# The second feed-forward weights split by casting and accumulating DMAs from GpSimd's queue

## The chip, the cores and the metric

The program runs on one core of one Trainium2 chip. The metric is the device time of one execution in microseconds (us). The engines are named as in the profile: PE (TensorE, with its weight loads shown apart as PEld), DVE (VectorE), ACT (ScalarE), POOL (GpSimd) and SP (SyncE, which here only issues DMAs).

## The reference

The program computes one layer of a decoder trunk for 512 tokens of 1024 channels, in float32. Cut to what matters:

```python
h = rms_norm(x, g_mix)
p = h @ w_in                       # 1024 x 7680, feeds three token mixers and three gates
y = [hgrn2_mix(...) @ w_branch[0], short_conv_mix(...) @ w_branch[1], spatial_gating_mix(...) @ w_branch[2]]
x = x + (sum of sigmoid(gate) * y) @ w_o          # 1024 x 1024
h2 = rms_norm(x, g_ffn)
x = x + square(relu(h2 @ w_ff1)) @ w_ff2          # 1024 x 4096, then 4096 x 1024
return rms_norm(x, g_final)
```

The second feed-forward weights are `w_ff2`. They reach the kernel as `w_2`, 32 blocks of 128 x 1024 float32, 512 KB each.

## The kernel before, in words

Every large product is done in three passes on PE. Each operand is written as a high part, which is the operand rounded to the type fp32r, and a low part, which is what the rounding left; `mm3` (lines 88 to 91) then adds high x high, high x low and low x high in one PSUM accumulator. So every block of weights must be split before PE can use it.

The work on PE is a list of units, run in the order of the list by the loop at line 858. A unit is 24 matmuls of 128 x 128 by 512 columns, plus what hooks add (`pre` hooks run before a unit's matmuls, `post` hooks after them). A unit that needs a new block of weights names a load. Loads are kept in one list with the unit ("slot") at which they are split, two units or more before their use.

For each load the loop does three things. `issue` (line 731) starts the DMA of a block into one of three `raw` buffers. At the load's slot `split_hi` (line 739) has ACT copy `raw` to the high part, and `split_lo` (line 749) has DVE subtract the high part from `raw` and write the low part. Four loads are issued ahead of the loop, and from then on each split is followed by one more issue; so a load is issued when the load two places before it is split. Most blocks go to the rotating buffers `wh` and `wl` (three of each). The blocks of `w_2` go to 16 fixed buffers `h0` to `h15` instead (`hslot`; block i takes buffers 2 x (i mod 8) and the next), since a block of `w_2` is used in four units.

All engines keep the order of the program in their queues. Within one unit that order is: `split_hi` for the loads of this slot; the evaluation of the unit before (`ev_...`, its first half); `split_lo`; the evaluation's second half; the other `pre` hooks; `issue`; the matmuls; the `post` hooks.

The feed-forward part begins with eight units that matter here; call them U0 to U7. U0 to U3 are the first four products with `w_1`, whose results stay in PSUM at first, because the row scale of the second norm is not known yet:

- At U0 the evaluation of the last output-projection unit (`ev_o`, line 609) ends with a POOL addition into the sum of squares `sgb` (line 625).
- At U1 `ffn_split` (line 635) splits that sum, on ACT and then DVE, and `ffn_ss` (line 639) multiplies it by ones on PE (lines 145 and 146), behind U1's matmuls.
- At U2 `ffn_rows` (line 643) makes the row scale `r2b`: a square root on ACT, a reciprocal on DVE, two products on POOL (lines 649 and 650), one more operation on DVE (line 652).
- At U3 `ffn_late` evaluates U0 to U2 (`ev_1`, line 660: DVE, ACT, ACT, DVE).

In the slots of these units stand, in the order of the list: U0: `w_1` block 2; U1: `w_1` block 3, `w_2` block 0; U2: `w_1` 4, `w_2` 1; U3: `w_1` 5, `w_2` 2; U4: `w_2` 3, `w_1` 6; U5: `w_1` 7; U6 and on: `w_2` 4 to 7. `w_1` block n is used in unit Un for n up to 7; `w_2` blocks 0 to 3 are first used in U8.

From U4 on the part repeats with a period of eight units (seven groups): four units with `w_1`, four with `w_2`, and in its slots two loads of `w_1`, four of `w_2`, two of `w_1`. The four blocks of `w_2` of one group are used in the last four units of the next group. The last four blocks are used in the closing part (line 894 on), which starts three units after the last of them is split.

Of the kernel before, what the change touches and what calls it, by code (L numbers as in the profile page):

```python
# [8 lines left out]
F32R = mybir.dt.float32r  # L9
U8 = mybir.dt.uint8  # L10
AF = mybir.ActivationFunctionType
ALU = mybir.AluOpType
# [24 lines left out]
def trunk_kernel(ctx: ExitStack, tc, xT, w_f, w_t, w_bc, w_a, w_o, w_1, w_2, vecs, rows, w_sg, cst, lmask, out):  # L37
    nc = tc.nc
# [5 lines left out]
    dve, act, pool, pe = nc.vector, nc.scalar, nc.gpsimd, nc.tensor  # L44
# [3 lines left out]
    def nm(s):  # L48
        uid[0] += 1
        return f"{s}_{uid[0]}"  # L50

    def ct(shape, name, dt=F32):
        return cp.tile(shape, dt, name=name, tag=name)

    def xslot(i, dt):
        return rp.tile([P, S], dt, tag=f"x{i}", name=nm("x"))

    def zslot(i, dt):
        return rp.tile([P, S], dt, tag=f"z{i}", name=nm("z"))

    def hslot(i, dt):
        return rp.tile([P, 2 * S], dt, tag=f"h{i}", name=nm("h"))

    def acc():
        return pa.tile([P, S], F32, tag="acc", name=nm("acc"))

    def f(ap):
        return ap.bitcast(F32)

    def tt(e, o, a, b, op):  # L70
        return e.tensor_tensor(out=o, in0=a, in1=b, op=op)  # L71

    def raw():
        return wp.tile([P, 2 * S], F32, tag="raw", name=nm("raw"))
# [18 lines left out]
    def cs(k, n=P):  # L93
        return slice(k * n, (k + 1) * n)

    # constants
    vec = ct([P, V_N], "vec")
    cons = ct([P, C_N], "cons")
    ident = cons[:, C_ID:C_ID + P]
# [12 lines left out]
    def tmp(w=S, dt=F32):  # L112
        return wp.tile([P, w], dt, tag="tmp", name=nm("tmp"), bufs=6)

    def rsqrt_cols(src, n, inv, eps, dst):
        """dst[:, :n] = (src * inv + eps) ** -0.5"""
        a = wp.tile([P, 4], F32, tag="ra", name=nm("ra"), bufs=4)
        dve.tensor_scalar(out=a[:, :n], in0=src, scalar1=inv, scalar2=eps, op0=ALU.mult, op1=ALU.add)
        tt(pool, dst[:, :n], a[:, :n], mhalf[:, :n], ALU.pow)
# [49 lines left out]
    units = []  # L169
# [5 lines left out]
    loads, when = [], {}  # L175
# [14 lines left out]
            return a  # L190
        return unit(w_f[j], mm, ev)

    # recurrence: decays, keys, queries
    def ev_f(h, a):
        kk[h] = zslot(2 * h, F32)
        A[h] = zslot(2 * h + 1, F32)
        hs = [hslot(h * 4 + i, F32) for i in range(4)]
        names = ("QA", "t1", "QB", "y", "q", "R", "go", "att")
        d = {n: hs[i // 2][:, cs(i % 2, S)] for i, n in enumerate(names)}
        heads.append(d)  # L200
        fp = d["QA"]
        tt(dve, fp, a, rb, ALU.mult)
        act.activation(kk[h], fp, AF.Sigmoid, scale=-1.0)
        act.activation(d["t1"], fp, AF.Abs)
        pool.memset(d["att"], 0.0)
# [55 lines left out]
            dve.tensor_scalar(out=d["y"], in0=d["y"], scalar1=al[:, h:h + 1], scalar2=cl[:, h:h + 1], op0=ALU.add, op1=ALU.max)  # L261
            tt(dve, A[h], d["y"], d["t1"], ALU.add)

    # recurrence: interactions at distance scale m = 2 ** l
    def halves(ap, m):
        v = ap.rearrange("p (b two m) -> p b two m", two=2, m=m)
        if m == 1:
            v = v[:, :, :, 0]
            return v[:, :, 0], v[:, :, 1]
        return v[:, :, 0, :], v[:, :, 1, :]  # L270
# [51 lines left out]
            mk = lm[:, cs(l)].unsqueeze(1).to_broadcast([P, 4, P])  # L322
            dve.copy_predicated(v4(d["att"]), mk, v4(d["ps"]))

    # recurrence: blocks of 128 through the state
    def far_prep(pair):
        for h in pair:
            d = heads[h]
            act.activation(d["y"][:, :3 * P], d["R"][:, :3 * P], AF.Exp)
            act.activation(d["t1"][:, P:], A[h][:, P:], AF.Exp)  # L330
        for h in pair:
            d = heads[h]
            tt(dve, d["QA"][:, :3 * P], kk[h][:, :3 * P], d["y"][:, :3 * P], ALU.mult)
            tt(dve, d["QB"][:, P:], d["q"][:, P:], d["t1"][:, P:], ALU.mult)
# [39 lines left out]
    def mix_norm(pair):  # L374
        for h in pair:
            d = heads[h]
            ss, r = col4(), col4()
            for b in range(4):
                act.activation(d["QA"][:, cs(b)], d["ps"][:, cs(b)], AF.Square, accum_out=ss[:, b:b + 1])
            rsqrt_cols(ss, 4, 1.0 / P, EPS, r)  # L380
            d["r"] = r
# [17 lines left out]
            zt[0][h] = (zslot(2 * h, F32R), zslot(2 * h + 1, F32R))  # L399
            split(d["t1"], *zt[0][h])  # L400

    # spatial gate
    def v_mm(j):
        def mm(w):
            if j == 0:
                part["v"] = [acc() for _ in range(4)]
            a4 = part["v"]
            for k2 in range(2):
                k = 2 * j + k2
                for t in range(4):  # L410
                    mm3(a4[t], xh[k][:, cs(t)], xl[k][:, cs(t)], w[0][:, cs(k2, S)], w[1][:, cs(k2, S)], k == 0, k == KD - 1)
        return mm
# [19 lines left out]
    def v_norm():  # L432
        r = col4()
        rsqrt_cols(mv[:, :, 1], 4, 1.0, LN_EPS, r)
        for t in range(4):
            dve.tensor_scalar(out=vln[t], in0=vln[t], scalar1=mv[:, t, 0:1], scalar2=r[:, t:t + 1], op0=ALU.subtract, op1=ALU.mult)
# [42 lines left out]
        zt[2][g] = (zslot(16 + 2 * g, F32R), zslot(17 + 2 * g, F32R))  # L479
        split(part["sv", g], *zt[2][g])  # L480

    # short convolution
    def ev_cg(c, a):
        y = tmp()
        part["cy"] = y
        tt(dve, y, a, rb2, ALU.mult)
# [18 lines left out]
        yield  # L505
        tt(dve, lo, y, f(hi), ALU.subtract)

    # gates, branch outputs, merge
    def ev_gate(d, n, a):
        g = tmp()  # L510
        part[n] = g
        tt(dve, g, a, rb, ALU.mult)
        act.activation(g, g, AF.Sigmoid)
# [19 lines left out]
        tt(dve, mt[:, S:], part[0], f(mt[:, :S]), ALU.subtract)  # L533
        mg.append((mt[:, :S], mt[:, S:]))

    # order of the units of tensor work
    for h in range(NH):
        proj(4 + h, lambda a, h=h: ev_f(h, a))
    for h in range(NH):
# [57 lines left out]
        at(pre, 19 + g, sg_split, g)  # L597
    at(pre, 21, go_sig)

    # output projection, residual, second norm  # L600
    x2, x2h, x2l = [], [], []

    def reload_x():
# [37 lines left out]
        ones_mm(part["c2"], part["qh"], part["ql"])  # L641

    def ffn_rows():
        """-2 * (mean square + eps) ** -0.5, on every partition"""
        a, r, t = tmp(), tmp(), tmp()
        act.activation(r, part["c2"], AF.Sqrt, scale=1.0 / D, bias=eps_c)
        dve.tensor_scalar(out=a, in0=part["c2"], scalar1=1.0 / D, scalar2=EPS, op0=ALU.mult, op1=ALU.add)
        dve.reciprocal(r, r)
        tt(pool, t, a, r, ALU.mult)
        tt(pool, t, t, r, ALU.mult)  # L650
        part["r2b"] = ct([P, S], "rb2")
        dve.scalar_tensor_tensor(out=part["r2b"], in0=t, scalar=-3.0, in1=r, op0=ALU.add, op1=ALU.mult)
# [1 line left out]
    def ffn_late():  # L654
        return [ev_1(i, held[i]) for i in range(3)]

    # feed-forward
    hid = {}

    def ev_1(i, a):  # L660
# [48 lines left out]
    at(pre, f0 + 1, ffn_split)  # L709
    at(post, f0 + 1, ffn_ss)  # L710
    at(pre, f0 + 2, ffn_rows)
    at(pre, f0 + 3, ffn_late)
    for g in range(1, NG):
# [13 lines left out]
    raws, ws = {}, {}  # L727
    order = [x for s in sorted(when) for x in when[s]]
    issued = [0]

    def issue():
        if issued[0] < len(order):
            src, n, _ = loads[order[issued[0]]]
            r = raw()
            nc.sync.dma_start(r[:, :n], src)
            raws[order[issued[0]]] = r
            issued[0] += 1

    def split_hi(i):
        _, n, tiles = loads[i]  # L740
        if tiles:
            hi, lo = (hslot(t, F32R) for t in tiles)
        else:
            hi = wp.tile([P, 2 * S], F32R, tag="wh", name=nm("wh"))
            lo = wp.tile([P, 2 * S], F32R, tag="wl", name=nm("wl"))
        act.activation(hi[:, :n], raws[i][:, :n], AF.Copy)  # L746
        ws[i] = (hi, lo)

    def split_lo(i):
        n = loads[i][1]  # L750
        hi, lo = ws[i]
        tt(dve, lo[:, :n], raws.pop(i)[:, :n], f(hi[:, :n]), ALU.subtract)

    held = []
    with tc.manual_schedule():
        # warm the tensor engine's clock and the activation tables while the first loads run
        dve.memset(ones, 1.0)
        pool.memset(mhalf, -0.5)
        nc.scalar.dma_start(vec, vecs)
# [2 lines left out]
        warm = acc()  # L762
        for i in range(WARM):
            pe.matmul(warm[:, :P], ones, ones, start=True, stop=True)

        # x: load, scale by the gain, split, sum of squares; the recurrence's value rows, token-major
        xr = [zslot(k, F32) for k in range(KD)]
        rw = []
        for k in range(KD):
# [17 lines left out]
        for k in range(KD + 1):  # L787
            if k < KD:
                hi = xslot(2 * k, F32R)
                lo = xslot(2 * k + 1, F32R)  # L790
# [26 lines left out]
            if k == KD:  # L817
                cps = acc()
                col_sums(cps, sq_tot)
                rsqrt_cols(cps[:, :4], 4, 1.0 / D, EPS, rstd)  # L820
                dg = diag(rstd)
                dh = ones_hi(dg)
                dl = ones_lo(dg, dh)
# [3 lines left out]
            hi, lo = xh[j], xl[j]  # L827
# [6 lines left out]
            if j in (3, 5, 6):  # L834
                issue()
            if j == 5:
                split_hi(order[0])
                split_lo(order[0])
        issue()
        dve.tensor_copy(lm, lf[:, :7 * P])  # L840
        for t in range(4):
# [11 lines left out]
        for x in when[-1]:  # L853
            split_hi(x)
            split_lo(x)

        prev = None
        for i in range(len(units)):
            hooks = pre.get(i, [])
            todo = when.get(i, [])  # L860
            for x in todo:
                if x not in raws:
                    issue()
                split_hi(x)
# [12 lines left out]
            for x in todo:  # L877
                split_lo(x)
# [12 lines left out]
                fn(*a)  # L891
        prev[0](prev[1])

        # last group of the feed-forward, by token halves, and the final norm
        g = NG - 1
        n2 = S // 2

# [75 lines left out]
        warm = acc()  # L973
# [60 lines left out]
```

## Time and profile before

| what | value |
|---|---|
| runs | 857.92, 860.74, 861.56 us, median 860.74 us |
| profiled execution, first to last instruction (its span) | 859.3 us |
| PE busy | 847.2 us, 99% of the span |
| DVE, ACT, POOL busy | 473.6, 322.3, 140.4 us (55%, 38%, 16%) |
| DMA | 83.59 MB, 97 GB/s over the span |

The page gives one profiled execution; its span is the only time of it that is shown, and the runs are other executions of the same program. Busy is the time in which an engine executes instructions, not the time for which it is needed. Of two engines that are busy at once, the one whose next instruction others wait for sets the time; that is read from the chain of waits and from the timelines of the single engines, not from the shares.

### The profile page before, as it was taken

How to read it: one execution, taken by the hardware profiler on the slowest of the kernel's cores; microseconds unless marked ns; L12 is line 12 of the kernel's file. 1: busy time of each engine (PE TensorE's matmuls, PEld its weight loads, DVE VectorE, ACT ScalarE, POOL GpSimd, SP SyncE). 2: the span in 40 equal slices, each digit the busy share in tenths (PEclk: the TensorE clock that was granted, in tenths of full speed). 3: DMA queues.
4: the chain of work that ended last, by engine and by line, in shares of the span. 5: the costliest groups of instructions: out<-in, count | busy, mean ns of one | idle time of the engine just before them, and what ended most of it. 6: DMA issues, size and time to landing. Idle time of an engine off the chain costs nothing.

```text
span 859.3 us, 10105 instructions
## 1 busy us (share of the span) xinstructions
PE 847.2 (99%) x3990; PEld 706.8 (82%) x3990; DVE 473.6 (55%) x623; ACT 322.3 (38%) x491; POOL 140.4 (16%) x152
## 2 busy tenths in 40 slices
PE   8999899999999999999999999999999999999997
PEld 7888788888888888888888888888888888888896
DVE  7456989978564444544445458444444444444424
ACT  6567355354333232323223446232232323232222
POOL 4313455661210000000001310000000000000034
PEclk9999999999999999999999999999999999999999
DMA  8331222212122323232235234222223232322002
GB/s 302 118 99 50 84 88 75 74 50 98 50 75 86 110 86 111 86 96 100 86 110 208 92 131 149 96 98 98 98 98 98 98 98 98 98 91 90 17 1 99
DMA packets 26256, 83.59 MB, mean 97 GB/s; under 512 B 3040, under 2 KB 3424, under 8 KB 26208
## 3 DMA queue, kind: packets, MB, share of 16 engines
q1 hardware_dynamic: 26064, 82.91, 29.1%
q8 instruction: 31, 0.51, 0.2%
q14 instruction: 17, 0.14, 0.1%
q10 hardware_dynamic: 144, 0.03, 0.0%
HBM read 80.83 MB, written 2.10 MB: 97 GB/s over the span
## 4 chain that ended last, share of the span: by engine, by line
PE 91%; DVE 3%; ACT 3%; issue 2%; DMA 0%; SPq 0%; POOL 0%; DVEq 0%; ACTq 0%
PE acc L89 28%; PE acc L91 28%; PE acc L90 28%; PE acc L317 3%; PE acc L833 1%; DVE wl L71 1%; DVE h L71 1%; ACT h L248 1%; DVE h L261 0%; DMA z<-xT 0%; ACT wh L746 0%; ACT h L252 0%; PE acc L469 0%; PE acc L370 0%; DVE h L298 0%
## 5 line engine op out<-in xcount | busy, mean ns | idle before, releaser
L89 PE MATMUL acc<-x,wh 128*128 128x512 f32 x672 | 265.5, 395 | 0.0
L90 PE MATMUL acc<-x,wh 128*128 128x512 f32 x672 | 262.7, 391 | 0.0
L91 PE MATMUL acc<-x,wl 128*128 128x512 f32 x672 | 262.7, 391 | 0.0
L746 ACT ACTIVATE wh<-raw 128x1024 fp32r<-128x1024 f32 (+1 forms) x112 | 115.0, 1028 | 377.0 <-PE acc L90 247.4
L71 DVE TENSOR_TENSOR wl<-raw,wh 128x1024 fp32r<-128x1024 f32 (+1 forms) x118 | 151.4, 1284 | 24.9 <-ACT wh L746 24.8
L91 PEld LDWEIGHTS acc<-x,wl 128*128 128x128 f32 x672 | 126.2, 188 | 28.6
L89 PEld LDWEIGHTS acc<-x,wh 128*128 128x128 f32 x672 | 126.3, 188 | 26.5
L90 PEld LDWEIGHTS acc<-x,wh 128*128 128x128 f32 x672 | 126.3, 188 | 26.4
L71 DVE TENSOR_TENSOR z<-z,acc 128x512 f32<-128x512 f32 (+1 forms) x80 | 50.6, 634 | 109.8 <-PE acc L91 109.8
L89 PE MATMUL acc<-z,h 128*128 128x512 f32 (+1 forms) x288 | 105.5, 366 | 0.0
L90 PE MATMUL acc<-z,h 128*128 128x512 f32 (+1 forms) x288 | 105.2, 365 | 0.0
L91 PE MATMUL acc<-z,h 128*128 128x512 f32 (+1 forms) x288 | 105.2, 365 | 0.0
L71 POOL TENSOR_TENSOR tmp<-tmp,tmp 128x512 f32<-128x512 f32 (+1 forms) x27 | 31.5, 1166 | 218.6 <-DVE tmp L71 186.9
L662 DVE SCALAR_TENSOR_TENSOR tmp<-acc,rb 128x512 f32<-128x512 f32 x32 | 21.9, 690 | 76.0 <-PE acc L91 76.0
L71 DVE TENSOR_TENSOR tmp<-acc,rb 128x512 f32<-128x512 f32 x28 | 19.3, 691 | 80.5 <-PE acc L91 80.5
L89 PEld LDWEIGHTS acc<-z,h 128*128 128x128 f32 x288 | 54.3, 189 | 8.8
L90 PEld LDWEIGHTS acc<-z,h 128*128 128x128 f32 x288 | 54.3, 189 | 8.8
L91 PEld LDWEIGHTS acc<-z,h 128*128 128x128 f32 x288 | 54.3, 189 | 8.7
L917 POOL TENSOR_SCALAR z<-z,vec 128x256 f32<-128x256 f32 x12 | 5.8, 484 | 312.5 <-ACT tmp L911 312.5
L663 ACT ACTIVATE tmp<-tmp 128x512 f32<-128x512 f32 x32 | 20.1, 628 | 69.2 <-DVE tmp L662 69.2
L71 DVE TENSOR_TENSOR h<-raw,h 128x1024 fp32r<-128x1024 f32 x32 | 38.9, 1217 | 0.0
L89 PE MATMUL acc<-z,wh 128*128 128x512 f32 x96 | 37.8, 394 | 0.0
(184 smaller groups left out, 984.4 us busy)
## 6 DMA issues: line engine op xcount, KB each, us to landing
raw<-w SPq DMA_DIRECT2D x64, 512.0 KB, 3.3
raw<-w_f SPq DMA_DIRECT2D x52, 512.0 KB, 3.3
raw<-w_bc SPq DMA_DIRECT2D x8, 512.0 KB, 3.3
raw<-w_o SPq DMA_DIRECT2D x8, 512.0 KB, 3.3
z<-xT SPq DMA_DIRECT2D x15, 256.0 KB, 4.3
raw<-w_t SPq DMA_DIRECT2D x4, 512.0 KB, 3.3
raw<-w_a SPq DMA_DIRECT2D x8, 256.0 KB, 2.5
out<-x SPq DMA_DIRECT2D x8, 256.0 KB, 2.1
```

The costliest lines, as they stand in the source:

```text
L71: return e.tensor_tensor(out=o, in0=a, in1=b, op=op)
L89: pe.matmul(o, lh, rh, start=start, stop=False)
L90: pe.matmul(o, lh, rl, start=False, stop=False)
L91: pe.matmul(o, ll, rh, start=False, stop=stop)
L248: act.activation(d["t1"], d["t1"], AF.Exp, scale=-1.0)
L317: pe.matmul(ps[:, cs(b)], kl[:, cs(b)], qk[:, cs(b)], start=True, stop=True)
L662: dve.scalar_tensor_tensor(out=t, in0=a, scalar=0.0, in1=part["r2b"], op0=ALU.max, op1=ALU.mult)
L663: act.activation(t, t, AF.Square, scale=0.5)
L746: act.activation(hi[:, :n], raws[i][:, :n], AF.Copy)
L833: pe.matmul(a4[t], lh, rh, start=j == 0 and rnd == 0, stop=j == KD - 1 and rnd == 2)
L917: pool.tensor_scalar(out=xv, in0=xv, scalar1=vcol(V_GFIN + d), scalar2=0.0, op0=ALU.mult, op1=ALU.add)
```

## The change

For the 32 blocks of `w_2` (and for no others) `issue` no longer loads into `raw` from SP's queue. It takes the two `h` buffers at once, and a DMA in POOL's queue reads the block from memory and writes the high part, casting float32 to fp32r. At the slot, `split_hi` has ACT write minus the high part into the low buffer, and a second DMA in POOL's queue reads the block from memory again and adds it to the low buffer. `split_lo` does nothing for these blocks, so DVE's 32 subtractions go. The other hunks of the diff only take out comments.

```diff
     def issue():
         if issued[0] < len(order):
-            src, n, _ = loads[order[issued[0]]]
-            r = raw()
-            nc.sync.dma_start(r[:, :n], src)
-            raws[order[issued[0]]] = r
+            src, n, tiles = loads[order[issued[0]]]
+            if tiles:
+                hi, lo = (hslot(t, F32R) for t in tiles)
+                pool.dma_start(hi, src)
+                ws[order[issued[0]]] = (hi, lo)
+                raws[order[issued[0]]] = None
+            else:
+                r = raw()
+                nc.sync.dma_start(r[:, :n], src)
+                raws[order[issued[0]]] = r
             issued[0] += 1
 
     def split_hi(i):
-        _, n, tiles = loads[i]
+        src, n, tiles = loads[i]
         if tiles:
-            hi, lo = (hslot(t, F32R) for t in tiles)
+            hi, lo = ws[i]
+            act.activation(lo, f(hi), AF.Copy, scale=-1.0)
+            pool.dma_start(lo, src, accum_op=ALU.add)
+            return
         else:
...
     def split_lo(i):
         n = loads[i][1]
+        if loads[i][2]:
+            return
         hi, lo = ws[i]
         tt(dve, lo[:, :n], raws.pop(i)[:, :n], f(hi[:, :n]), ALU.subtract)
```

## Rows read from the trace of the kernel before

**Rows 1.** The page: busy time, share of span, instructions; 40 slices in tenths.
```profile
PE 847.2 (99%) x3990; PEld 706.8 (82%) x3990; DVE 473.6 (55%) x623; ACT 322.3 (38%) x491; POOL 140.4 (16%) x152
PEclk9999999999999999999999999999999999999999
```

**Rows 2.** The page: shares of the chain that ended last, by engine.
```profile
PE 91%; DVE 3%; ACT 3%; issue 2%; DMA 0%; SPq 0%; POOL 0%; DVEq 0%; ACTq 0%
```

**Rows 3.** Windows: length, busy us (instructions) of PE, PEld, DVE, ACT, POOL; clock, DMA share, GB/s.
```profile
495.00:539.00 44.00, 44.00 (x194) 36.11 (x193) 29.35 (x32) 25.05 (x32) 4.38 (x3) 1.00 0.46 144
561.00:605.00 44.00, 44.00 (x194) 36.25 (x194) 20.14 (x24) 12.88 (x16) 0.00 (x0) 1.00 0.29 96
605.00:649.00 44.00, 44.00 (x195) 36.27 (x194) 20.20 (x25) 12.88 (x16) 0.00 (x0) 1.00 0.29 96
```

**Rows 4.** Groups of instructions, 495 to 840 us: busy us, mean ns, idle before, releaser.
```profile
L71 DVE TENSOR_TENSOR h<-raw,h 128x1024 fp32r<-128x1024 f32 x32 | 38.9, 1217 | 0.0
L746 ACT ACTIVATE h<-raw 128x1024 fp32r<-128x1024 f32 x32 | 33.4, 1045 | 0.0
```

**Rows 5.** POOL in order of time, 495 to 530 us: start, length, line, tiles.
```profile
497.46 1.80 POOL L71 TENSOR_TENSOR sgb<-sgb,tmp 128x512 f32<-128x512 f32 x1 [3.70 <-ACT tmp L624]
514.19 2.67 POOL L71 TENSOR_TENSOR tmp<-tmp,tmp 128x512 f32<-128x512 f32 x2 [14.93 <-DVE tmp L648]
```

**Rows 6.** ACT in order of time, units U1 to U4.
```profile
501.58 1.04 ACT L746 ACTIVATE h<-raw 128x1024 fp32r<-128x1024 f32 x1
502.53 0.62 ACT L136 ACTIVATE tmp<-sgb 128x512 fp32r<-128x512 f32 x1
...
507.08 1.04 ACT L746 ACTIVATE h<-raw 128x1024 fp32r<-128x1024 f32 x1
508.14 1.28 ACT L646 ACT_TABLE_LOAD   x1
509.44 0.69 ACT L646 ACTIVATE tmp<-acc,eps_c 128x512 f32<-128x512 f32 x1
...
512.99 1.04 ACT L746 ACTIVATE h<-raw 128x1024 fp32r<-128x1024 f32 x1
...
521.98 1.05 ACT L746 ACTIVATE h<-raw 128x1024 fp32r<-128x1024 f32 x1
524.08 1.06 ACT L746 ACTIVATE wh<-raw 128x1024 fp32r<-128x1024 f32 x1 [1.06 <-DMA raw<-w]
```

**Rows 7.** DVE in order of time, units U1 to U4.
```profile
503.99 0.68 DVE L71 TENSOR_TENSOR tmp<-sgb,tmp 128x512 fp32r<-128x512 f32 x1
...
510.77 3.34 DVE L648 RECIPROCAL tmp<-tmp 128x512 f32<-128x512 f32 x1
...
519.42 1.21 DVE L71 TENSOR_TENSOR wl<-raw,wh 128x1024 fp32r<-128x1024 f32 x1
...
525.23 1.22 DVE L71 TENSOR_TENSOR wl<-raw,wh 128x1024 fp32r<-128x1024 f32 x1
```

**Rows 8.** PE in order of time: end of U1, third matmul of U5, start of U6.
```profile
506.33 0.39 PE L146 MATMUL acc<-tmp,ones_r 128*128 128x512 f32 x1
...
523.49 0.39 PE L91 MATMUL acc<-x,wl 128*128 128x512 f32 x1
...
528.52 0.39 PE L89 MATMUL acc<-x,wh 128*128 128x512 f32 x1
528.75 0.39 PE L90 MATMUL acc<-x,wh 128*128 128x512 f32 x1
528.99 0.39 PE L91 MATMUL acc<-x,wl 128*128 128x512 f32 x1
```

**Rows 9.** ACT and DVE in order of time, in a later group; PE at the closing part.
```profile
566.74 1.06 ACT L746 ACTIVATE wh<-raw 128x1024 fp32r<-128x1024 f32 x1 [15.42 <-PE acc L90]
568.89 1.04 ACT L746 ACTIVATE h<-raw 128x1024 fp32r<-128x1024 f32 x1
...
579.88 1.04 ACT L746 ACTIVATE h<-raw 128x1024 fp32r<-128x1024 f32 x1
...
567.83 1.23 DVE L71 TENSOR_TENSOR wl<-raw,wh 128x1024 fp32r<-128x1024 f32 x1 [0.17 <-ACT wh L746]
...
823.67 0.28 PE L89 MATMUL acc<-z,h 128*128 128x256 f32 x1
```

**Rows 10.** DMA issues: tile, queue, count, KB each, median us from issue to landing.
```profile
raw<-w SPq DMA_DIRECT2D x64, 512.0 KB, 3.3
z<-xT SPq DMA_DIRECT2D x15, 256.0 KB, 4.3
h<-w_t SPq DMA_DIRECT2D x2, 256.0 KB, 5.9
```

**Rows 11.** The page: GB/s moved by the DMA engines in 40 slices.
```profile
GB/s 302 118 99 50 84 88 75 74 50 98 50 75 86 110 86 111 86 96 100 86 110 208 92 131 149 96 98 98 98 98 98 98 98 98 98 91 90 17 1 99
```

## The prediction

> **What bounds the kernel now.** I read the page's busy shares first, then the chain of waits, then windows over the feed-forward part, and last the timelines of the engines where that part begins. PE is busy 99% of the span at full granted clock [rows 1], and the chain that ended last is PE for 91% [rows 2]. In the feed-forward part no hole is left at all: in windows of 44 us PE is busy 44.00 us, at clock 1.00, with 194 or 195 matmuls in each [rows 3]. So nothing that DVE, ACT or a queue does there is on the path, and the change, which lies in that part alone, can take time away only by making PE's own matmuls quicker. It can add time wherever it makes PE wait. The question is which margins it uses up.
>
> **What goes.** DVE loses 32 subtractions of 1217 ns, 38.9 us [rows 4]. DVE is busy 20 of 44 us in a later group [rows 3], all of it beside PE, so this is worth 0. The 32 loads of `w_2` leave SP's queue and the three `raw` buffers, so the loads of `w_1` start earlier; no PE instruction waits for them, worth 0. ACT keeps its 32 instructions: the copy of 1045 ns [rows 4] now reads the high buffer instead of `raw`. I cost it the same.
>
> **What comes.** 64 DMAs in POOL's queue, 32 that cast and 32 that accumulate, and two new waits: ACT's copy waits for the cast DMA, and the accumulating DMA waits in POOL's queue for that copy. Queued behind the first are ACT's splits of `w_1`, the square root and the evaluations; behind the second are the next cast DMA and, in U2, the two POOL products of `ffn_rows`.
>
> *In the six later groups* this has room. The first cast DMA of a group waits only for the `h` buffers, which PE leaves at about 561.5 us (the ACT instruction of the second unit starts at 566.74 [rows 9], one unit of 24 x 0.229 = 5.5 us later than that). ACT copies at 568.89, 7.4 us later. The third cast DMA is queued behind the accumulation that follows this copy, at about 569.9, and is wanted at 579.88 [rows 9], 10 us later. The results are used a group later, or three units (16 us) later in the last one. I cost these groups at 0 while a DMA lands in under about 8 us and the queue keeps its pace.
>
> *In the first group* they stand in a chain, because the loads come two to a slot and POOL and ACT also make the row scale. Let La to Ld be the times from POOL's turn to landing of the cast DMAs of blocks 0 to 3, and g the time that POOL spends on an accumulating DMA before it turns to the next.
>
> - Block 0's cast DMA is issued at U0 behind POOL's addition, which ends at 497.46 + 1.80 = 499.26 [rows 5].
> - It lands La later; ACT's copy takes 1.04 [rows 6]; the accumulating DMA takes g; block 1's cast DMA lands Lb later; ACT copies again, 1.04.
> - Only then does ACT come to its table load and square root, 2.01 (508.12 to 510.13 [rows 6]). The reciprocal on DVE ends 3.98 after that (514.11 [rows 7]), and POOL's two products 2.75 later (516.86 [rows 5]).
> - Block 2's cast DMA is issued in U2 after these hooks, so it stands behind both products. It lands Lc later, ACT copies, 1.04, the accumulation takes g, block 3's cast DMA lands Ld later, ACT copies, 1.04. (ACT's six evaluation instructions fit into g + Ld.)
> - Behind that copy stands ACT's split of `w_1` block 6. From its start to the end of DVE's low part a split takes 569.06 - 566.74 = 2.32 [rows 9].
>
> The fixed terms are 499.26 + 1.04 + 1.04 + 2.01 + 3.98 + 2.75 + 1.04 + 1.04 + 2.32 = 514.48. U6 wants this low part at its third matmul, 528.99 [rows 8]; before, it was there at 525.23 + 1.22 = 526.45 [rows 7]. So PE waits La + Lb + Lc + Ld + 2g - 14.5 us, if that is positive. What PE loses there is never given back, since there is no hole behind it.
>
> No row shows a cast or accumulating DMA or POOL's queue, so I bound them. Below: the plain 512 KB load from SP's queue, 3.3 us [rows 10], since the same bytes come from the same memory, and g = 0: 13.2 - 14.5, no wait. Above: 6.6 for each, two such transfers end to end, which exceeds the 5.9 of loads in a crowd [rows 10], and g = 1.8, a POOL instruction here [rows 5]: 26.4 + 3.6 - 14.5 = 15.5 us. I take 3.8 for a cast DMA by itself, halfway between 3.3 and the 4.3 of the reload of x [rows 10], since the size is that of the 3.3 row but the queue is POOL's and the data are cast. I add 1.6, half of 3.3, to Lb and Ld, which follow an accumulating DMA into the same engines. And g = 1, near the middle of its bounds. The sum is 3.8 + 5.4 + 3.8 + 5.4 + 2.0 - 14.5 = **5.9 us**.
>
> The same chain has two earlier ends. `ffn_split` on ACT and DVE is then done at 499.26 + 3.8 + 1.04 + 0.62 + 0.75 = 505.5, before PE wants the second half at 506.33 [rows 6 to 8]: no wait while La stays under 4.6. The low part of `w_1` block 5 was done at 520.63 for 523.49 [rows 7, 8], 2.9 us of margin, against a square root that ends 503.35 + La + Lb + g - 510.13 = 3.4 us later: about 0.6 of the 5.9 would be seen at U5, the rest at U6. These are parts of the same total, not additions.
>
> The Trainium skill, DMA: Bandwidth & Descriptors, section on the anatomy of one DMA on the SWDGE (gpsimd) path, fits a DMA from that queue as 2.0 us plus the bytes over 436 GB/s. As an estimate that makes 3.2 us for 512 KB, close to the 3.3 of the plain queue; with the same additions the wait would be 3.5 us instead of 5.9. No run here shows POOL's queue yet. Against the change, Collectives: The Full Stack says (stop 4 and the comparison of reduce-scatter) that an add in the DMA path costs not its arithmetic but a second source read; by that the accumulating DMA moves twice its size, which speaks for the addition to Lb and Ld.
>
> The profiled execution has a span of 859.3, so it becomes 865.2. The median of the runs, 860.74, lies 1.4 above this span; the forecast for the median is 860.74 + 5.9 = **866.6 us**.
>
> **The rivals.**
>
> *Hidden.* If a cast DMA lands like a plain one and accumulation hardly delays the next, the sum of the six terms stays below 18.8 and PE waits less than 4.3 us. With 3.3 each and g = 1 it waits 0.7: 861.4. For it: the DMA engines are used at 0.29 to 0.46 in this part [rows 3]. Against it: it needs all four landings near their lower bound. Not slower, 861 to 865.
>
> *The queue sets the pace.* 64 DMAs from 499.3 to the closing part at 823.67 [rows 9] leave 5.07 us for each. If they don't overlap and each takes more than that, PE waits in every group. At 6.6 the last would land at 499.3 + 422.4 = 921.7, and with the closing 35.6 the span is 957, the median 959. Against it: in the first slice of the span the engines moved 302 GB/s [rows 11]; at that rate 512 KB take 1.7 us, and twice that for an accumulation makes 2.6 on average, half of the limit.
>
> *Faster.* The mechanism would be that PE's reads of SBUF are slowed by DVE's two-input subtractions, so that without the 32 of them the matmuls follow each other more closely. 0.5% needs 1.3% of the 329 us from U0 to the closing part. Against it: the matmuls at 528.52, 528.75 and 528.99 start 0.23 apart [rows 8], and the count per 44 us is 194 where DVE is busy 29 us and 194 where it is busy 20 [rows 3]. Price at most some 4 to 5 us: 856.
>
> **How the numbers follow.** The chain in the first group (2 to 16 us) gets 0.58, of which 0.53 above 4.3 us; hidden 0.31; the queue as the bound 0.07; faster 0.04, of which 0.03 beyond 0.5%. 0.5% is about what a measurement of this kernel can tell from no change. That makes slower 0.60, same 0.37, faster 0.03. The range goes from just below no change, 860.0, to 878.0, the upper bound of the chain (876.3) and a little; outside are most of the queue's case, the faster one and a tenth of the rest.
>
> **What would show it.** In the changed profile: PE has one hole near the start of U6 of some 5 us and perhaps a small one at U5, both ended by the low part of `wl`, and none in later groups; DVE has no instruction on `h` from `raw`; ACT waits for DMA at its first four copies into `h`; POOL's two products of `ffn_rows` start later than 514.19. The prediction fails if these landings total under 16.5 us with g, if holes recur every eight units, or if PE's matmuls change their spacing.

## The result, and the profile after

The changed kernel takes 871.76 us (median of 4 runs, 871.11 to 874.04), the kernel before 860.16 us in the same set (4 runs, 857.92 to 861.56). The ratio is 1.0133, 95% interval 1.0105 to 1.0160: slower by 11.6 us. The forecast was 866.6 us, slower by 5.9.

The page of the changed kernel, against [rows 1, 2]. Busy time and share of the span; PE, clock and DMA in 40 slices of 21.8 us; the chain by engine.

```profile
PE 853.2 (98%) x3990; PEld 710.4 (81%) x3990; DVE 439.1 (50%) x591; ACT 321.4 (37%) x491; POOL 184.7 (21%) x216
...
PE   9999899999999999999999997999999999999996
...
PEclk9999899999999999999999998999999999999998
DMA  8331222213122332333244256855555555553502
...
PE 86%; DVE 4%; ACT 4%; DMA 3%; issue 2%; POOL 0%; SPq 0%; DVEq 0%; POOLq 0%; ACTq 0%
```

DVE lost its 32 subtractions (623 to 591 instructions, 473.6 to 439.1 us), POOL has 64 more, ACT is where it was. DMA is now 3% of the chain. One slice in the middle of the feed-forward part is weak: PE's digit there is 7 and the clock's 8, where both were 9 before. (The fifth slice and the last, outside that part, have an 8 of the clock too, and 9 before.) Windows over that part show the same, against [rows 3]:

```profile
480.00:520.00 40.00, 40.00 (x177) 32.82 (x176) 16.80 (x17) 16.34 (x20) 10.23 (x8) 1.00 0.47 133
520.00:560.00 40.00, 33.70 (x132) 26.48 (x131) 17.10 (x24) 20.12 (x27) 11.09 (x14) 0.91 0.74 186
560.00:600.00 40.00, 40.00 (x177) 32.99 (x176) 14.37 (x19) 12.23 (x17) 5.69 (x8) 1.00 0.61 157
600.00:640.00 40.00, 40.00 (x177) 32.95 (x177) 14.26 (x18) 8.95 (x12) 4.80 (x7) 1.00 0.59 151
```

From 520 to 560 us PE runs 132 matmuls where a full window holds 177, and is idle for 6.3 us; before and after that it misses nothing. PE's timeline in that window, against [rows 8] (the third matmul of U5, the last of U5, and the first three of U6; the brackets give the idle time before, and what ended it):

```profile
527.18 0.50 PE L91 MATMUL acc<-x,wl 128*128 128x512 f32 x1 [2.29 <-DVE wl L71]
...
533.71 0.40 PE L91 MATMUL acc<-x,wl 128*128 128x512 f32 x1
537.59 0.50 PE L89 MATMUL acc<-x,wh 128*128 128x512 f32 x1 [3.48 <-ACT wh L755]
537.93 0.39 PE L90 MATMUL acc<-x,wh 128*128 128x512 f32 x1
538.85 0.72 PE L91 MATMUL acc<-x,wl 128*128 128x512 f32 x1 [0.53 <-DVE wl L71]
```

These are the two holes of the forecast, at U5 and U6, each ended by a split of `w_1`. The chain that leads to them is on POOL's and ACT's timelines. POOL, against [rows 5] (line 736 is the cast DMA, 750 the accumulating one):

```profile
498.70 1.80 POOL L71 TENSOR_TENSOR sgb<-sgb,tmp 128x512 f32<-128x512 f32 x1 [3.70 <-ACT tmp L624]
500.44 0.78 POOL L736 DMA_DIRECT2D h<-w  x1
505.66 0.89 POOL L750 DMA_DIRECT2D h<-w  x1 [4.45 <-ACT h L749]
506.22 0.90 POOL L736 DMA_DIRECT2D h<-w  x1
514.93 0.87 POOL L750 DMA_DIRECT2D h<-w  x1 [7.81 <-ACT h L749]
520.70 2.65 POOL L71 TENSOR_TENSOR tmp<-tmp,tmp 128x512 f32<-128x512 f32 x2 [4.90 <-DVE tmp L648]
523.30 0.60 POOL L736 DMA_DIRECT2D h<-w  x1
528.41 0.88 POOL L750 DMA_DIRECT2D h<-w  x1 [4.52 <-ACT h L749]
529.15 0.70 POOL L736 DMA_DIRECT2D h<-w  x1
```

ACT, against [rows 6] (line 749 is the copy into the low buffer):

```profile
504.28 1.06 ACT L749 ACTIVATE h<-h 128x1024 fp32r<-128x1024 f32 x1 [1.37 <-DMA h<-w]
...
513.57 1.06 ACT L749 ACTIVATE h<-h 128x1024 fp32r<-128x1024 f32 x1 [5.17 <-DMA h<-w]
514.65 1.28 ACT L646 ACT_TABLE_LOAD   x1
515.94 0.69 ACT L646 ACTIVATE tmp<-acc,eps_c 128x512 f32<-128x512 f32 x1
...
527.05 1.06 ACT L749 ACTIVATE h<-h 128x1024 fp32r<-128x1024 f32 x1 [9.47 <-DMA h<-w]
...
535.53 1.06 ACT L749 ACTIVATE h<-h 128x1024 fp32r<-128x1024 f32 x1 [3.87 <-DMA h<-w]
536.50 1.04 ACT L755 ACTIVATE wh<-raw 128x1024 fp32r<-128x1024 f32 x1
```

The four copies wait for the four cast DMAs, and each accumulating DMA waits in POOL's queue for the copy. PE loses speed too. In windows of 5 us the granted clock (the column after the engines) falls to 0.76 to 0.90 around the holes; the matmuls behind each hole start 0.43 us apart for about 3 us, which is the lower of the clock's two levels (1.2 GHz), and 0.23 apart before and after:

```profile
520.00:525.00 5.00, 4.89 (x22) 3.68 (x20) 2.19 (x4) 0.00 (x0) 3.12 (x3) 1.00 0.10 16
525.00:530.00 5.00, 2.81 (x10) 2.28 (x11) 2.80 (x4) 2.88 (x5) 1.43 (x2) 0.87 0.55 195
530.00:535.00 5.00, 4.10 (x14) 2.95 (x12) 2.00 (x4) 1.63 (x3) 0.00 (x0) 0.79 0.92 209
535.00:540.00 5.00, 1.89 (x5) 1.26 (x6) 2.43 (x4) 4.10 (x5) 1.96 (x3) 0.90 0.33 47
540.00:545.00 5.00, 5.00 (x18) 3.96 (x18) 2.47 (x4) 2.56 (x4) 0.00 (x0) 0.76 1.05 337
545.00:550.00 5.00, 5.00 (x24) 4.10 (x23) 1.99 (x3) 3.24 (x5) 2.85 (x4) 1.00 1.03 265
```

To compare stretches, I read the starts of U0, U8, the closing part and the first of PE's last four matmuls (line 149 before; "last PE" below) from PE's timeline of each profiled execution. Differences in us:

```
kernel            U0 starts  U0 to U8  U8 to closing  closing to last PE  last PE to end  span
before              495.11     44.40      284.16            28.51             7.16       859.34
after               496.34     54.73      284.18            28.51             8.51       872.27
first 4 plain       497.22     44.41      284.16            28.50             7.86       862.15
first 4 only        495.62     54.32      284.18            28.51             7.51       870.14
casts together      495.14     44.41      284.16            28.50             8.52       860.73
block 6 ahead       496.72     48.62      284.17            28.50             8.51       866.52
cast only           494.21     44.81      284.17            28.51             7.23       858.93
accumulate only     494.32     44.41      284.16            28.50             7.24       858.63
cast 2 early        494.69     47.47      284.17            28.51             8.51       863.35
holes filled        493.91     53.30      284.16            28.50             8.52       868.39
```

Of the 12.93 us between the two profiled executions 10.33 lie between U0 and U8. Counted as what PE's starts lose against their usual spacing of 0.23, these are 2.46 of waiting at U5, 1.72 of slow clock behind it, 3.65 and 0.80 of waiting at U6, and 1.69 of slow clock behind that. From U8 to the closing part, where 26 of the 32 blocks are split, nothing changes by more than 0.02 us. 1.35 lie behind the last matmuls, and 1.23 ahead of U0, where all these programs do the same work and still differ by up to 3.3; part of the 1.23 is the clock, which over 87 to 109 us was 0.92 before and 0.84 after.

### The profile page after: what moved, and what is told of

It is laid out like the page before. It is cut to its first block, busy times and chain, and to the rows that moved or that the text cites. A ratio compares the mean times of both kernels' runs of the same rounds, so it can differ in the third digit from the quotient of the medians.

```text
span 872.3 us, 10126 instructions
## 1 busy us (share of the span) xinstructions
PE 853.2 (98%) x3990; PEld 710.4 (81%) x3990; DVE 439.1 (50%) x591; ACT 321.4 (37%) x491; POOL 184.7 (21%) x216
## 4 chain that ended last, share of the span: by engine, by line
PE 86%; DVE 4%; ACT 4%; DMA 3%; issue 2%; POOL 0%; SPq 0%; DVEq 0%; POOLq 0%; ACTq 0%
PE acc L89 27%; PE acc L91 27%; PE acc L90 27%; PE acc L317 3%; DMA h<-w 2%; PE acc L844 1%; DVE wl L71 1%; DVE h L71 1%; ACT wh L755 1%; DMA z<-xT 1%; ACT h L248 1%; DVE h L261 0%; ACT h L252 0%; PE acc L370 0%; PE acc L469 0%
## 5 line engine op out<-in xcount | busy, mean ns | idle before, releaser
L750 POOL DMA_DIRECT2D h<-w x32 | 27.9, 871 | 173.0 <-ACT h L749 173.0
L71 DVE TENSOR_TENSOR z<-tmp,z 128x512 fp32r<-128x512 f32 x40 | 27.6, 690 | 35.6 <-ACT z L666 35.6
L749 ACT ACTIVATE h<-h 128x1024 fp32r<-128x1024 f32 x32 | 33.6, 1049 | 28.0 <-DMA h<-w 28.0
L736 POOL DMA_DIRECT2D h<-w x32 | 23.1, 732 | 91.1 <-PE acc L90 90.4
```

The source lines that it names most:

```text
L736: pool.dma_start(hi, src)
L749: act.activation(lo, f(hi), AF.Copy, scale=-1.0)
L750: pool.dma_start(lo, src, accum_op=ALU.add)
```

## The experiments

**Which blocks?** Two kernels split the 32 blocks between the old path and the new:

```diff
+    plain = {w2l[i] for i in range(NF) if i < 4}      # in the second kernel: i >= 4
...
-            if tiles:
+            if tiles and order[issued[0]] not in plain:
```

> Blocks 0 to 3 of w_2 take the old path (load into raw, copy on ACT, subtraction on DVE); the other 28 keep the two DMAs from POOL's queue. Chain theory (all the loss sits where the feed-forward part begins, U1 to U7): back to before, 859 to 862 us, no hole in PE after U0. Rival A (every DMA from POOL's queue costs PE a little, spread over all groups): 28/32 of the loss stays, about 870 us. Rival B (a fixed cost of using POOL's queue at the start or the end of the program): 861.5 to 863 us, with the excess outside the feed-forward part.

Measured: 861.83 us against 860.56 in the same set, ratio 1.0016 (1.0005 to 1.0026). U0 to U8 takes 44.41 us, as before, with 56 DMAs still in POOL's queue. This refutes the loss spread over all groups; the 1.3 us that stay are partly the 0.7 behind the last matmuls.

> The reverse: only blocks 0 to 3 of w_2 go by POOL's queue, the other 28 by the old path. Chain theory: nearly the whole loss, 869 to 872 us, with the two holes of PE at U5 and U6. Rival A: 4/32 of the loss, about 861.6 us. Rival B: 861.5 to 863 us.

Measured: 872.31 us, ratio 1.0132 (1.0118 to 1.0146). Four blocks of 32 carry the loss: U0 to U8 takes 9.92 us more than before, against 10.33 with all 32. The holes are the same two, as its waits of PE show (engine, tile and line, what it waited for: us in all, times, longest):

```profile
PE acc L89 <- ACT wh L758: 3.7, 1, 3.7
...
PE acc L91 <- DVE wl L71: 2.5, 2, 2.0
```

**Is it the order or the transfers?** Three kernels keep all 64 DMAs and change only where some instruction stands. First, the four cast DMAs of the first group are issued together at U0:

```diff
+                for x in ([w2l[j] for j in range(4)] if i == w2l[0] else [i]):
+                    if x not in ws:
...
+                        pool.dma_start(hi, loads[x][0])
```

> All 64 DMAs stay, but the four cast DMAs of blocks 0 to 3 are issued together at U0, so that none stands behind an accumulating DMA or behind the two POOL products of ffn_rows. Chain theory: the landings are no longer added up; the last lands by about 510 us, no wait of PE, 859 to 863 us. Rival C (POOL's queue is short of bandwidth where it meets the loads of w_1, so that the order does not matter): still 868 us or more, since four transfers then meet at once.

Measured: 862.61 us, ratio 1.0021 (1.0011 to 1.0032); U0 to U8 44.41 us, no hole. So bandwidth was not short: the same transfers, closer together, cost PE nothing. POOL's queue now reads as follows; all four casts stand ahead of the first accumulation and of the products:

```profile
499.24 2.39 POOL L739 DMA_DIRECT2D h<-w  x4
504.47 0.91 POOL L753 DMA_DIRECT2D h<-w  x1 [2.84 <-ACT h L752]
508.46 0.87 POOL L753 DMA_DIRECT2D h<-w  x1 [3.08 <-ACT h L752]
514.23 2.66 POOL L71 TENSOR_TENSOR tmp<-tmp,tmp 128x512 f32<-128x512 f32 x2 [4.90 <-DVE tmp L648]
```

Second, in U4's slot block 6 of `w_1` is split ahead of block 3 of `w_2`:

```diff
-    for i in range(GF):
+    for i in range(GF - 1):
         load_2(f0 + 1 + i, i)
...
             w1l[g * GF + 2 + j] = load(b0 + j, w_1[g * GF + 2 + j])
+            if g == 1 and j == 0:
+                load_2(b0, 3)
```

> Only the order in one slot is changed: block 6 of w_1 is split ahead of block 3 of w_2, so ACT's copy for U6 no longer stands behind the fourth cast DMA. Chain theory: the hole at U6 goes (3.65 and 0.80 us of waiting and 1.69 us of slow clock behind it), the hole at U5 stays (2.46 and 1.72): about 865.5 us. Rival C: 871 us, since the same transfers meet.

Measured: 866.43 us (863.96 to 868.30), ratio 1.0068 (1.0053 to 1.0083). The hole at U5 stays with 2.10 us, the one at U6 shrinks to 0.78, and U0 to U8 takes 4.22 us more than before. The expected 4.18 had 1.72 of slow clock in it; here the clock stayed at 1.00 and small waits at U6 and U7 made up the sum, so the total was met partly by chance.

Third, in U2 the cast DMA of block 2 is issued ahead of the two products of `ffn_rows`:

```diff
+            if i == f0 + 2:
+                for x in todo:
+                    issue()
             for fn, a in hooks:
```

> Only the place of one issue is changed: in U2 the cast DMA of block 2 is issued ahead of the two POOL products of ffn_rows. Chain theory: it lands some 5 us earlier and ACT's copy of it waits no more; the hole at U6 goes, the one at U5 stays: about 865.5 us. Rival D (the POOL products do not matter, the chain is all in the transfers): 870 to 872 us.

Measured: 865.77 us, ratio 1.0055 (1.0038 to 1.0072); U0 to U8 is 3.07 us longer than before. The hole at U5 is unchanged and the one at U6 is gone but for 0.19, again at clock 1.00:

```profile
525.52 0.51 PE L91 MATMUL acc<-x,wl 128*128 128x512 f32 x1 [2.28 <-DVE wl L71]
...
531.50 0.50 PE L91 MATMUL acc<-x,wl 128*128 128x512 f32 x1 [0.19 <-DVE wl L71]
```

So a POOL instruction of 1.3 us, twice, was a link of the chain, by its place in the queue.

**Which half?** One kernel keeps only the cast DMA (the low part comes from `raw` by DVE), one only the accumulating DMA (ACT makes the high part from `raw`, DVE writes its negative); the comments are added here:

```diff
+                pool.dma_start(hi, src)                 # cast only; the block goes to raw too
...
+            dve.tensor_scalar(out=lo, in0=f(hi), scalar1=-1.0, scalar2=None, op0=ALU.mult)
+            pool.dma_start(lo, loads[i][0], accum_op=ALU.add)   # accumulate only
```

> One half of the change: the high part is written by the cast DMA from POOL's queue; the low part comes from raw by DVE's subtraction as before, so there is no accumulating DMA and no ACT copy for w_2. Chain theory: a cast DMA no longer stands behind an ACT copy and an accumulation, so the landings overlap; no wait of PE, 859 to 862 us, although ACT is rid of 32 instructions (33 us) too. Rival (ACT's time matters): faster than before, below 857 us.

Measured: 861.91 us against 860.89, ratio 1.0012 (1.0001 to 1.0023). Not faster, though ACT has 32 instructions less.

> The other half: the high part is made as before from raw by ACT; DVE writes minus the high part, and the accumulating DMA from POOL's queue adds the block. ACT waits for no DMA of POOL's queue. Chain theory: no wait of PE, 859 to 862 us. Rival A (accumulating DMAs slow PE or the other loads in all groups): 864 us or more.

Measured: 860.28 us, ratio 0.9990 (0.9981 to 1.0000), as before. Neither half costs anything worth naming. The loss needs both: the accumulation that waits for ACT's copy, the copy that waits for a cast, and the next cast behind that accumulation.

These two also separate the engine time of the kinds, that is the time that a DMA's packets took, summed and divided by 16 engines. The DMA queues of the cast-only kernel (packets, MB, share of 16 engines' span; q0 is POOL's queue), and then of the accumulate-only one:

```profile
q1 hardware_dynamic: 26064, 82.91, 28.5%
q0 software_dynamic: 4608, 16.78, 6.0%
```

```profile
q0 software_dynamic: 4608, 16.78, 11.5%
```

A cast of 512 KB takes 0.060 x 858.9 / 32 = 1.61 us of all engines, about as long as a plain load (0.285 x 858.9 us for 82.91 MB, 1.55 us for 0.524 MB). An accumulation takes 0.115 x 858.6 / 32 = 3.09, though the queue counts the same 16.78 MB for it.

**The clock.** 30 matmuls whose results nobody uses are put in front of U5 (10) and U6 (20); the comment is added here:

```diff
+            for _ in range(fill):                       # {5: 10, 6: 20}
+                pe.matmul(a, x2h[0][:, :P], x2h[0], start=True, stop=True)
```

> The changed kernel with 30 extra matmuls of 512 columns whose results are overwritten: 10 at the start of U5 and 20 at the start of U6, 6.9 us of extra work at full clock, put into the two holes. If the clock falls because PE stood idle: it stays at 1.00 and 2.5 to 3.4 us come back, 868.4 to 869.3 us, in spite of the extra work. If the clock falls for another reason (the DMA engines at a share of 0.9 to 1.05 there): no gain, 871.5 to 874 us.

Measured: 870.90 us, ratio 1.0112 (1.0092 to 1.0133). In its profile the clock is 1.00 in every 5 us window from 520 to 550, although the DMA share rises to 1.14 there, and U0 to U8 takes 53.30 us, 1.43 less than in the changed kernel, in spite of the extra work:

```profile
530.00:535.00 5.00, 4.70 (x21) 3.57 (x19) 0.52 (x1) 1.75 (x2) 0.40 (x1) 1.00 0.46 140
535.00:540.00 5.00, 4.16 (x17) 3.15 (x18) 4.42 (x6) 3.62 (x6) 1.57 (x3) 1.00 0.79 170
540.00:545.00 5.00, 5.00 (x24) 4.09 (x23) 1.74 (x3) 2.46 (x4) 1.43 (x2) 1.00 1.14 372
```

That speaks for idleness, not DMA traffic, as what lowered it, and so does the casts-together kernel, in which PE has no hole and the clock is 1.00 from 500 to 515 us at a DMA share of 1.00. But the gain was expected at 2.5 to 3.4 us. The lines of the changed kernel above give the reason: the slow clock after the first hole (1.72 us) ran while PE would have waited for the second hole's release anyway, and only the slow matmuls after the second hole (1.69 us) reached the end. On the medians, from two sets of runs, the gain is 0.9 us, and the two intervals overlap (1.0092 to 1.0133, and 1.0105 to 1.0160 for the changed kernel), so they do not show it. Nor does every hole lower the clock: it did not fall behind the 2.28 us in the kernel with block 2's cast issued early, nor behind the 2.10 with block 6 ahead, but it fell behind 2.29 in the changed kernel and behind 1.99 with the first four blocks only. What decides between these stays open.

## Why the prediction was right, and where its size was off

**Right: the mechanism, the place and the free parts.** PE had no hole to give back and none was gained; the later groups cost 0 (U8 to closing, 284.16 and 284.18); DVE's 38.9 us were worth 0; the loss stands at U5 and U6 of the first group. The hole at U6 was ended first by the high part (3.48 us) and then by the low part (0.53), where the forecast named the low part alone. The prediction also passed over blocks 4 to 7, which are in neither its first group nor its six later ones: of the 28.0 us that ACT waits for casts in the changed kernel (eight waits), 8.1 are at these four. No PE instruction waited for them, so the 0 was right there by margins that had not been worked out.

**The chain, term by term.** POOL's addition ends at 500.50 here. The cast DMAs land 3.78, 7.35, 3.70 and 6.38 us after their turn (504.28, 513.57 from 506.22, 527.05 from 523.35, 535.53 from 529.15), and POOL passes each accumulation 0.88 and 1.04 after the copy's end. The formula gives 21.21 + 1.92 - 14.5 = 8.6. PE's third matmul of U6 would have started at 528.99 + 1.23 = 530.22 in this execution and started at 538.85: 8.63 late. The fixed terms were all as read from before.

**Wrong: the size of Lb and Ld.** La and Lc were taken as 3.8 and were 3.8 and 3.7. Lb and Ld, the casts behind an accumulating DMA, were taken as 5.4 (an addition of 1.6) and were 7.35 and 6.38. The addition came from half of a plain load's landing time; what stands ahead in the engines is an accumulation of 3.1 us of engine time, and at Lb and Ld the addition was 3.6 and 2.6. The later groups of the same trace bear this out: from block 8 on a cast that POOL issues 0.56 us behind an accumulation lands 6.1 to 7.6 us after its issue, and the first cast of a group, with none ahead, 3.5 to 4.7. Loads of `w_1` run beside them (the one issued at 509.69 landed after 5.09 us instead of 3.3); how much of Lb is theirs is not shown. The two additions make 2.9 of the missing us. The same term makes the hole at U5 2.46 instead of 0.6. The estimate of 3.2 us by the Trainium skill's fit (DMA: Bandwidth & Descriptors, anatomy of one DMA on the SWDGE path) was half a microsecond short of the 3.7 and 3.8 of a cast with nothing ahead, and by it the forecast would have been farther off. The Trainium skill's rule that an add in the DMA path costs a second source read (Collectives: The Full Stack, the bandwidth ceiling) agrees with the 3.09 against 1.61.

**Missing: the clock.** No term was given to PE's clock after a hole, 1.69 us that count.

**Missing: behind the last matmuls,** 1.35 us. SP's waits at the end of the program show it; first the kernel before, then the changed one:

```profile
SPq L1029 <- PEq L1029: 0.6, 2, 0.4
```

```profile
SPq L1040 <- PEq L1040: 2.3, 2, 1.8
```

The end waits 1.7 us longer for PE's sequencer. From the last matmuls to the end it is 8.5 us in all five kernels in which all blocks take both DMAs, and 7.2 to 7.9 in the other five. These two waits of SP add up to 2.3 us in all five with 64 DMAs in POOL's queue, to 1.4 with 56, and to 0.6 or 0.7 with 32, 8 or none. So, with one profile of each kernel, it goes with the number of these DMAs; what PE's sequencer does there stays open. It is also most of what the casts-together kernel still loses.

The sum is 5.9 + 2.7 (landings and g) + 1.7 + 1.4 = 11.7, for 11.6 measured on the medians; the terms are those of two single executions. So the chain that was forecast accounts for 8.6 us, and 3.1 came from two terms that the sum did not have. The forecast was about half of what was measured, and it was the width of the range, 18 us, that held the result.

**The rivals.** *Hidden* was refuted by Lb and Ld: the six terms make 23.1, not less than 18.8. *The queue sets the pace* was refuted by the first four plain kernel: a cast and an accumulation together take 4.7 us of engine time per block, under the 10.1 that two times 5.07 allowed. *Faster* was refuted: the matmuls from U8 on keep their spacing.

## What to carry to other kernels

A new DMA in an in-order queue is priced by what stands ahead of it and who waits for it: follow the chain through every queue where the pipeline starts, for there the lead is shortest, and then the steady state by engine time. Here the cure is an order (all casts ahead of the first accumulation), not bandwidth, and it brings the changed kernel to 1.0021 of the one before; no version tried beats it by more than noise, since PE has no hole to fill in that part. Work taken off an engine that is beside the bound is worth nothing, and a hole in PE can cost more than its length, because the clock may fall behind it (1.69 us here).

## What the runs showed that I had not expected

An accumulating DMA lands 5.4 us (median; 5.1 to 7.8) after POOL's instruction and takes 1.9 times the engine time of a cast of the same block; a cast costs the engines what a plain load does. POOL spends 0.55 to 0.9 us per DMA, and starts the next 0.55 to 0.74 us after an accumulating one has started.
